# Differential attention on one core: the softmax, the transposes and the weighted sums of two tiles built as one pair

## The chip, the core and the metric

The kernel runs on one NeuronCore of a Trainium2 chip. The metric is the time of one execution in device microseconds (us); several executions are timed and the median is given. One further execution was recorded by the profiler, with its own time. The engines are named as in the profile: PE is TensorE, PEld its weight loads, DVE is VectorE, ACT is ScalarE, POOL is GpSimd, and SP issues most of the DMA transfers.

## The reference, cut to what matters

Two layers are applied to two independent requests of 512 tokens (x_prompt and x_sample, 1024 wide), each as x + mixer(RMSNorm(x)), and a last RMSNorm closes. Layer 1 is differential attention with 8 heads, layer 2 a bidirectional retention. The change lies in the attention of layer 1:

```
def block(qi):
    s = jnp.einsum('bqhd,bkhd->bhqk', qi, k).astype(f32)
    p = jax.nn.softmax(s, axis=-1).reshape(B, N_HEADS, 2, Q_BLOCK, S)
    a = (p[:, :, 0] - lam * p[:, :, 1]).astype(v.dtype)
    return jnp.einsum('bhqk,bkhe->bqhe', a, v)
...
o = rms_norm(o, subln_g, SUBLN_EPS) * (1.0 - lambda_init)
o = o.reshape(B, S, D_INNER) * jax.nn.silu(gate)
return o @ w_out
```

Each head has two score matrices, two softmaxes whose difference weighs the values (256 wide), a norm over the 256 columns, a gate, and the output projection to 1024 columns.

## The kernel before

All products are done in three passes over a high and a low part of each operand (`PASSES`), so one logical product is three matmuls. The program has four stages: the input projection of layer 1 (to about 617 us in the profile), the attention and its output projection (to about 1003 us), the input projection of layer 2 (to about 1480 us), and the retention with its output projection.

**Who sets the order.** The program text does not issue instructions. Each helper (`pe`, `act`, `dve`, `pool`, `axpy`, `dma`, `evac`) puts an operation on a `Plan` with a cost and with what it reads and writes. At the end `Plan.issue` lists the operations for all engines eight times with assumed costs and keeps the shortest plan. PE takes ready operations by their place in the last round's PE order, no further than 24 places ahead (`WINDOW`); the other engines take them by a due time computed backwards from PE. So the program text sets the first order and which buffers are taken in turn, the plan sets the rest, and a change in one stage can also move instructions in another.

**The attention, tile by tile.** A tile is (head, request, 128 queries): 64 tiles, numbered i, four to each head and request. For each tile:

- `scores` (L1202): two banks `sc`, three matmuls of 128x512 each.
- `row_max` (L1210): DVE takes the negated maximum of each bank.
- `exps` (L1220): ACT writes the exponentials into `p` and their sums into `sm`. When both are read the `sc` banks are free.
- `combine` (L1230 to L1239): POOL computes the factor of the second softmax (for the first four tiles DVE does), DVE forms the difference in place (L1236); on odd tiles POOL squares the sums of both tiles.
- `transp` (L1247): four 128x128 transposes into the only `tp` bank, a high part by ACT (L419) and a low part by DVE (L422) into the `aT` of the tile pair.
- `av` (L1267), once for two tiles: 24 matmuls of 128x256 into one of two `o` banks; then `weigh`: the gate (DVE L862), high and low part (L419, L422), the square (ACT L866) and the sum of its halves (DVE L867).
- `weighed`, once for two tiles: `norm_cols` transposes the squares (PE L874), sums them (ACT L878) and has POOL form the norm factor `rr` (L1279, L882). It owes four output pieces (`owe`).
- An output piece, `out_step` (L950, L955): six matmuls of 128x512 into one of three `pj` banks, and an `axpy` on DVE that scales by `rr` and adds to `xN`. The owed pieces wait in the list `todo`; `fill(n, lag)` puts up to n of them on the plan and leaves the last `lag` (`LAG` is 4) in the list. The weights of the pieces are split into parts twice for each head (L419 and L422 on 128x1024).

The loop before runs over single tiles: odd tiles start with an output piece and the weighted sum of the pair that ended two tiles ago, then come scores, softmax, an output piece, the transposes of the tile before, another piece, and on even tiles `weighed`.

Of the kernel before, what the change touches and what calls it, by code (L numbers as in the profile page):

```python
# [20 lines left out]
NH = 8  # L21
# [12 lines left out]
LAG = 4  # L34
# [221 lines left out]
def trunk_kernel(  # L256
# [15 lines left out]
    pj = ctx.enter_context(tc.tile_pool(name="pj", bufs=1, space=bass.MemoryType.PSUM))  # L272
# [8 lines left out]
    def view(pool, tag, i, size, shape, dt=F32):  # L281


        n = math.prod(shape[1:])
        if (tag, i) not in places:
            if size <= 32 and pool in (cp, wk):
                k = next(k for k, used in enumerate(gaps) if used + size <= PAD - 32)
                places[tag, i] = pads[k][:, gaps[k]:gaps[k] + size]
                gaps[k] += size
            else:  # L290
                places[tag, i] = pool.tile([P, size], F32, tag=f"{tag}{i}", name=f"{tag}_{i}", bufs=1)
        t = places[tag, i][0:shape[0], 0:n]
# [21 lines left out]
    def slot(n, shape, dt=F32R, shift=0):  # L314

        size = math.prod(shape[1:])
        at = None if n in (12, 13) or n >= 20 else n if n < 12 else n - 2
        if at is None:  # L320
            assert not shift
            cnt[0] += 1
            label = f"b_{cnt[0]}"
            return Buf(plan, f"b{n}", 1, lambda i: cp.tile(shape, dt, tag=f"b{n}", name=label))
        assert dt == F32R
        lo = at * 1024 + shift

        def make(i):
            t = arena[:, lo:lo + size]
            return t.rearrange("p (a b) -> p a b", a=shape[1]) if len(shape) == 3 else t  # L330
        b = Buf(plan, f"b{n}", 1, make)
        b.also = Buf(plan, f"edge{at + 1 if shift else at}", 1, None)
        return b
# [38 lines left out]
    def bank(tag, name=None):  # L372
        return Buf(plan, tag, BUFS[tag], lambda i: view(pj if tag == "pj" else sc, tag, i, S, [P, S]))
# [8 lines left out]
    def step(gen, n=1):  # L382
        for _ in range(n):
            next(gen, None)
# [24 lines left out]
    def pe(cost, fn, r, w, wait=0.0):  # L409
        plan.op("PE", cost, fn, r, w, wait=wait)  # L410
# [7 lines left out]
    def hi_of(n, dst, src, r, w):  # L418
        act(n, lambda: nc.scalar.copy(dst(), src()), r, w)  # L419

    def lo_of(n, dst, src, hi, r, w):
        dve(n, lambda: nc.vector.tensor_tensor(dst(), src(), hi().bitcast(F32), op=ALU.subtract), r, w)  # L422
# [409 lines left out]
    def projections(units, early):  # L832

        n = 2 + len(early)
        for u, place in zip(units[2:], early):
            u.early = place
        order = product_order(units, n)
        ready = 0
        for n, (u, op) in enumerate(order):
            while ready < len(order):  # L840
                v, p = order[ready]
                if sum(w.n_ws for w, _ in order[n:ready]) + v.n_ws > WS_BUFS:
                    break
                v.prep(p)
                ready += 1
            if units is first_units and n == len(order) - 1:
                u.product(op, 0)
                yield
                u.product(op, 1)
            else:  # L850
                u.product(op)
            u.evac(op)
            yield
# [34 lines left out]
    def load_qk(src, i, shift):  # L888
        t = slot(i, [P, 2, S], F32R, shift)
        dma(lambda: t.t.bitcast(F32), lambda: src[0][src[1]], [src[0]], [t], 512)  # L890
        return t

    def load_v(src, i, shift):
        out = []
        for a in range(2):
            t = slot(i + a, [P, NT, 256], F32R, shift)
            dma(lambda a=a, t=t: t.t.bitcast(F32), lambda a=a: src[a].rearrange("p (t e) -> p t e", t=NT),
                [src], [t], 512)
            out.append(t)
        return out  # L900

    def load_sg(src):
        t = os_t(F32, "sg")
        dma(lambda: t.t, lambda: src[:], [src], [t], 512)
        return t
# [5 lines left out]
    def fill(n, lag=0):  # L911
        for _ in range(n):
            if len(todo) > lag:
                todo.pop(0)()

    def new_xN(g, src):
        for t in range(NT):
            x = xN[g, t] = slot(20 + 4 * g + t, [P, D], F32)
            dma(lambda x=x: x.t, lambda t=t: src(t)[0], src(t)[1], [x], 512)
# [197 lines left out]
    for t in range(NT):  # L1117
        x_norm(0, t)
        x = xnat[0, t]
        half, at = t // 2, t % 2 * P  # L1120

        def turns(x=x, half=half, at=at):
            for k in range(4):
                lo = k % 2 * 256 + at
                nc.tensor.transpose(turned[half][k // 2][:, lo:lo + P], x[:, k * P:(k + 1) * P], ident.t)
        pe(0.44, turns, [ident, (x, 0)], [(ps, t) for ps in turned[half]])
        if half == 0:
            warm_up(2 if t else 1, [(x, 0)])
        if t % 2:
            for k in range(4):  # L1130
                first_piece(k, half)
# [3 lines left out]
    proj = projections(first_units, (12, 20, 22))  # L1135
# [41 lines left out]
    tiles = [(h, g, t) for h in range(NH) for g in range(NG) for t in range(NT)]  # L1177
    N = len(tiles)
# [3 lines left out]
    def fetch1(h, g, v=True):  # L1182
        for j in range(2):
            for which in range(2):
                qk[h, g, j, which] = load_qk((qk_d[0, which, h, g], j), 6 * which + 2 * g + j, 64 * which)
        if v:
            fetch1_v(h, g)

    def fetch1_v(h, g):
        vt[h, g] = load_v(v_d[0, h, g], 10 + 4 * g, 64)  # L1190
        sg[h, g] = load_sg(g_d[0, h, g])
# [48 lines left out]

    def transp(i):
        p, n = st[i]['p'], i % 2
        tp = bank("tp", "tpa")

        def fn():
            for j in range(NT):
                nc.tensor.transpose(tp[:, j * P:(j + 1) * P], p[:, 0, j * P:(j + 1) * P], ident.t)  # L1247
        pe(0.44, fn, [p, ident], [tp])
        if n == 0:
            st[i]['aT'] = [slot(4 + u, [P, NT, 256], F32R, 28) for u in range(2)]  # L1250
        aT, here = st[i - n]['aT'], slice(n * P, (n + 1) * P)
        src = lambda: tp.t.rearrange("p (j n) -> p j n", j=NT)
        hi_of(S, lambda: aT[0][:, :, here], src, [tp], [(aT[0], n)])
        lo_of(S, lambda: aT[1][:, :, here], src, lambda: aT[0][:, :, here], [tp, (aT[0], n)], [(aT[1], n)])
# [29 lines left out]
    def finished(g, t, i, half, n, key, end):  # L1284
# [11 lines left out]
        if (g, t) == (1, 1):  # L1296
            for place, n in ((2, 8),):
                todo[place:place] = [lambda: step(made, 1)] * n

    def at(f, i, n):  # L1300
        if 0 <= i < n:
            f(i)
# [3 lines left out]
    turns2 = itertools.chain(["sc", "o", "sc", "o"], itertools.cycle(["tp", "o"]))  # L1306
    made = make_b(1, x_source(1, xN, lambda g: next(turns2) if g else "pj"))

    for i in range(N + 5):
        if i % 2 and i > 2:  # L1310
            fill(1, LAG)
            at(av, i - 3, N)
        at(scores, i, N)
        at(row_max, i, N)
        at(exps, i, N)
        at(combine, i, N)
        if i < 5:
            step(proj, 1)
            if i in (2, 4):
                new_xN(i // 2 - 1, lambda t, g=i // 2 - 1: (xs[g][0, t * P:(t + 1) * P, :], []))  # L1320
            if i == 3:
                fetch1_v(0, 1)
        if not i % 2 or i < 3:
            fill(1, LAG)
        at(transp, i - 1, N)
        fill(1, LAG)
        if i % 2 == 0 and i > 3:
            at(weighed, i - 4, N)
        if i < N and i % 4 == 2 and i > 4:
            nh, ng = tiles[i][0:2]  # L1330
            if ng == 1 and nh + 1 < NH:
                fetch1(nh + 1, 0)
            elif ng == 0 and nh > 0:
                fetch1(nh, 1)
    while todo:
        fill(1)

# [5 lines left out]
    proj = projections(second_units, (12, 20, 22))  # L1343
# [275 lines left out]
```

## Time and profile before

| | |
|---|---|
| timed executions | 1798.52, 1798.78, 1799.33 us; median 1798.78 |
| profiled execution | 1797.39 us, of which the span from first to last instruction is 1795.2 |
| busy in the span | PE 1784.5, PEld 1562.0, DVE 1482.9, ACT 897.9, POOL 156.4 us |
| mean granted clock of TensorE | 0.999 |
| moved by DMA | 328.81 MB, 183 GB/s over the span |

The profiled execution is 1.39 us below the median of the timed ones. A busy time is the sum of an engine's instructions; those of PE overlap, so its pace is read from starts. Times of rows count from the start of the span.

### The profile page before, as it was taken

To read this page: it belongs to the slowest core of one execution; us is meant where nothing else is said; L and a number is where in the kernel's file an instruction comes from. 1 tells how busy PE (TensorE), PEld (TensorE's weight loads), DVE (VectorE), ACT (ScalarE), POOL (GpSimd) and SP (SyncE) were. 2 spreads that over 40 slices of the span, in tenths; PEclk is the share of its full clock that TensorE was granted. 3 is DMA by queue.
4 is the path that set the end of the run, shared out by engine and by line. 5 is a ranking of instruction groups with operands and counts; after the bars stand their busy time and mean duration, and the time that the engine had idled before them with its cause. 6 is when DMAs were issued, how large, how long until landed. Compare 5 with 4: busy or idle time off the path is not lost.

```text
span 1795.2 us, 27855 instructions
## 1 busy us (share of the span) xinstructions
PE 1784.5 (99%) x10321; PEld 1562.0 (87%) x10321; DVE 1482.9 (83%) x2340; ACT 897.9 (50%) x1865; POOL 156.4 (9%) x315
## 2 busy tenths in 40 slices
PE   9999999999999999999999999999999999999998
PEld 7889889898988888888888888898989988888887
DVE  8968788778699888888888897777887967888887
ACT  8754344343443565455555876444444454444446
POOL 1000000000000022222222200000000000111113
PEclk9999999999999999999999999999999999999999
DMA  6444554555545695454454524465647459664652
GB/s 219 141 136 141 165 163 148 191 162 153 187 124 183 209 336 200 161 186 169 168 181 140 200 71 142 141 211 164 210 137 240 142 191 409 260 230 176 232 213 94
DMA packets 162767, 328.81 MB, mean 183 GB/s; under 512 B 12724, under 2 KB 76872, under 8 KB 162632
## 3 DMA queue, kind: packets, MB, share of 16 engines
q1 hardware_dynamic: 162304, 326.71, 53.4%
q8 instruction: 81, 1.33, 0.3%
q14 instruction: 54, 0.44, 0.1%
q10 hardware_dynamic: 328, 0.34, 0.1%
HBM read 209.55 MB, written 117.44 MB: 182 GB/s over the span
## 4 chain that ended last, share of the span: by engine, by line
PE 95%; DVE 3%; ACT 1%; DMA 1%; issue 0%; POOL 0%; POOLq 0%; ACTq 0%; DVEq 0%
PE pj L637 21%; PE pj L950 19%; PE sc L637 11%; PE pj L647 10%; PE o L637 8%; PE o L1267 5%; PE sc L1202 5%; PE sc L647 5%; PE o L1444 2%; PE o L647 2%; PE tp L1247 2%; PE sc L1400 1%; PE tp L1424 1%; PE o L1452 1%; DVE ws L422 1%
## 5 line engine op out<-in xcount | busy, mean ns | idle before, releaser
L950 PE MATMUL pj<-ws,arena 128*128 128x512 f32 x1542 | 388.5, 395 | 0.0
L950 PEld LDWEIGHTS pj<-ws,arena 128*128 128x128 f32 x1542 | 277.6, 188 | 50.9 <-ACT m L404 0.2
L637 PE MATMUL pj<-b,ws 128*128 128x512 f32 x1080 | 263.3, 390 | 0.5 <-DVE e L698 0.5
L637 PEld LDWEIGHTS pj<-b,ws 128*128 128x128 f32 x1080 | 201.2, 188 | 42.2 <-issue 0.9
L955 DVE SCALAR_TENSOR_TENSOR b<-pj,pad,b 128x512 f32<-128x512 f32 (+1 forms) x257 | 190.2, 745 | 18.8 <-PE pj L950 17.9
L422 DVE TENSOR_TENSOR ws<-st,ws 128x512 fp32r<-128x512 f32 (+1 forms) x192 | 148.0, 775 | 63.2 <-ACT ws L419 56.4
L419 ACT CAST ws<-st 128x512 fp32r<-128x512 f32 (+1 forms) x192 | 132.0, 692 | 130.6 <-PE pj L637 41.9
L422 DVE TENSOR_TENSOR ws<-raw,ws 128x512 fp32r<-128x512 f32 (+2 forms) x165 | 142.0, 864 | 65.8 <-ACT ws L419 56.8
L637 PE MATMUL sc<-arena,ws 128*128 128x512 f32 x768 | 185.2, 389 | 0.0
L637 PE MATMUL o<-arena,ws 128*128 128x512 f32 x744 | 178.1, 390 | 0.0
L419 ACT CAST ws<-raw 128x512 fp32r<-128x512 f32 (+2 forms) x165 | 125.9, 768 | 90.2 <-PE o L637 48.1
L637 PEld LDWEIGHTS sc<-arena,ws 128*128 128x128 f32 x768 | 143.9, 188 | 29.8
L637 PEld LDWEIGHTS o<-arena,ws 128*128 128x128 f32 x744 | 138.5, 188 | 28.6 <-DVE arena L484 0.3
L637 PE MATMUL pj<-arena,ws 128*128 128x512 f32 x636 | 156.2, 390 | 0.0
L637 PEld LDWEIGHTS pj<-arena,ws 128*128 128x128 f32 x636 | 118.5, 188 | 24.2
L1220 ACT ACTIVATE b<-sc,pad 128x512 f32<-128x512 f32 x128 | 88.1, 691 | 79.2 <-DVE pad L1210 78.2
L690 ACT COPY c<-pj 128x512 f32<-128x512 f32 x104 | 60.8, 586 | 122.9 <-PE pj L637 69.0
L647 PE MATMUL pj<-ws,b 128*128 128x256 f32 x960 | 116.9, 275 | 0.0
L647 PEld LDWEIGHTS pj<-ws,b 128*128 128x128 f32 x960 | 113.3, 188 | 0.6
L1202 PE MATMUL sc<-arena 128*128 128x512 f32 x384 | 102.1, 393 | 0.0
L1267 PEld LDWEIGHTS o<-arena 128*128 128x128 f32 x768 | 93.2, 188 | 2.6
L1267 PE MATMUL o<-arena 128*128 128x256 f32 x768 | 93.7, 277 | 0.0
(223 smaller groups left out, 2862.6 us busy)
## 6 DMA issues: line engine op xcount, KB each, us to landing
qk<-os SPq DMA_DIRECT2D x192, 256.0 KB, 3.5
arena<-qk SPq DMA_DIRECT2D x96, 512.0 KB, 5.2
raw<-in_da_w_in_dram SPq DMA_DIRECT2D x64, 512.0 KB, 5.1
v<-os SPq DMA_DIRECT2D x64, 512.0 KB, 4.9
arena<-v SPq DMA_DIRECT2D x64, 512.0 KB, 4.2
raw<-in_ret_w_in_dram SPq DMA_DIRECT2D x48, 512.0 KB, 4.5
os<-g SPq DMA_DIRECT2D x32, 512.0 KB, 7.7
g<-e SPq DMA_DIRECT2D x48, 256.0 KB, 5.6
```

The lines of the kernel that those rows point to most:

```text
L419: act(n, lambda: nc.scalar.copy(dst(), src()), r, w)
L422: dve(n, lambda: nc.vector.tensor_tensor(dst(), src(), hi().bitcast(F32), op=ALU.subtract), r, w)
L637: nc.tensor.matmul(ps.t, a[u][0]()[:, k, :], bt[k][:, v, :], start=(opens and k == 0 and i == 0), stop=(k == 3 and i == 2), skip_group_che ...
L647: nc.tensor.matmul(ps[:, (t % 2) * 256:(t % 2) * 256 + 256], bt[k][:, v, t * P:(t + 1) * P], a[u][0]()[:, k, :], start=(opens and t % 2 == ...
L690: act(S, lambda c=c, ps=ps: nc.scalar.copy(c.t, ps.t), [ps], [c])
L950: nc.tensor.matmul(ps[:, here], o[a][:, e, t * P:(t + 1) * P], u[b][:, e, here], start=(m == 0), stop=(m == 5))
L955: axpy(n, lambda half=half, here=here, ps=ps: nc.vector.scalar_tensor_tensor(half, ps[:, here], rr[:, t % 2:t % 2 + 1], half, op0=ALU.mult ...
L1202: nc.tensor.matmul(s.t, q[:, a, t * P:(t + 1) * P], k[:, b, :], start=(n == 0), stop=(n == 2))
L1220: act(840, lambda j=j, s=s, m=m: nc.scalar.activation(p[:, j, :], s.t, AF.Exp, bias=m.t, accum_out=sm[:, 2 * j + n:2 * j + n + 1]), [s, m] ...
L1247: nc.tensor.transpose(tp[:, j * P:(j + 1) * P], p[:, 0, j * P:(j + 1) * P], ident.t)
L1267: nc.tensor.matmul(o[:, e * 256:(e + 1) * 256], v[b][:, j, e * P:(e + 1) * P], aT[a][:, j, :], start=(n == 0), stop=(n % 12 == 11), skip_g ...
L1444: nc.tensor.matmul(o[:, e * 256:(e + 1) * 256], v_[v][:, 2 * c + j, e * P:(e + 1) * P], a_[:, u, j * 256:(j + 1) * 256], start=(e == 0 and ...
```

## The change

It touches `transp` and the loop over the tiles. Tiles 0 to 5 keep the order of before. From tile 6 on the loop takes two tiles at once: scores and softmax of the even tile, two output pieces, scores and softmax of the odd tile, two output pieces, the weighted sum of the pair before, the transposes of both tiles behind each other, then the transposes of the squares of an earlier pair. The transposes of odd tiles go to a `pj` bank, which the output pieces use too. How many pieces stay in the list rises from 0 at tile 10 to 4 at tile 18. The counts of projection steps in the first five tiles are 1, 1, 2, 1, 0 in place of five times 1. Loads for the next head are put on the plan at the same tiles as before, at the end of the pair. No instruction is added or left out.

```
     def transp(i):
         p, n = st[i]['p'], i % 2
-        tp = bank("tp", "tpa")
+        tp = bank("pj" if n else "tp", "tpa")
...
+    FIRST = 6
...
-    for i in range(N + 5):
-        if i % 2 and i > 2:
-            fill(1, LAG)
-            at(av, i - 3, N)
+    def soften(i):
         at(scores, i, N)
         at(row_max, i, N)
         at(exps, i, N)
         at(combine, i, N)
...
+    GIVE = {0: 1, 1: 1, 2: 2, 3: 1}
...
+    for i in range(FIRST, N + 4, 2):
+        soften(i)
+        lag = max(0, min(LAG, i // 2 - 5))
+        fill(2, lag)
+        if i == FIRST:
+            transp(i - 1)
+        soften(i + 1)
+        fill(2, lag)
+        at(av, i - 2, N)
+        at(transp, i, N)
+        at(transp, i + 1, N)
+        at(weighed, i - 4, N)
+        fetch_next(i)
```

What the plan makes of it on PE, from a weighted sum (L1267) on, in the middle of the attention. Before, in the names `sc`, `o`, `tp` and `pj` are banks with their number, `b` the softmax tile that is transposed, `m` a square, `ws` output weights:

```order
L1267 MATMUL o_1_332<-arena_72 128x256 x24
L1202 MATMUL sc_0_248<-arena_72 128x512 x3
L1202 MATMUL sc_1_329<-arena_72 128x512 x3
L1247 MATMUL tp_0_293<-ident_0_240,b_43_5777 128x128 x4
L950 MATMUL pj_1_341<-ws_2_77,arena_72 128x512
L950 MATMUL pj_1_341<-ws_3_79,arena_72 128x512
```

And the same place after:

```order
L1267 MATMUL o_1_332<-arena_72 128x256 x24
L1247 MATMUL tp_0_293<-ident_0_240,b_43_5799 128x128 x4
L1247 MATMUL pj_0_289<-ident_0_240,b_44_5832 128x128 x4
L874 MATMUL o_0_296<-ident_0_240,m_1_441 128x128 x2
L1202 MATMUL sc_0_248<-arena_72 128x512 x3
L1202 MATMUL sc_1_329<-arena_72 128x512 x3
L950 MATMUL pj_1_341<-ws_0_73,arena_72 128x512
L950 MATMUL pj_1_341<-ws_1_75,arena_72 128x512
```

The two runs of transposes of a pair have become one run of ten behind the weighted sum; behind it follow in a fixed round six score matmuls, twelve of two output pieces, six of scores, twelve of two pieces, and the next weighted sum.

On DVE, from the gate of a weighted sum (L862) on; `c` is the gated sum, `pad` holds maxima and factors, `arena` the parts for PE. Before:

```order
L862 TENSOR_TENSOR c_1_514<-o_0_296,os_1_367 128x512
L1210 TENSOR_REDUCE pad_1_76<-sc_1_329 128x1
L867 TENSOR_TENSOR m_3_466<-m_3_466 128x256
L422 TENSOR_TENSOR arena_72<-tp_0_293,arena_72 128x4x128
L955 SCALAR_TENSOR_TENSOR b_36_228<-pj_1_341,pad_2_78,b_36_228 128x512
L1210 TENSOR_REDUCE pad_1_76<-sc_0_248 128x1
L422 TENSOR_TENSOR arena_72<-c_1_514,arena_72 128x2x256
L1236 SCALAR_TENSOR_TENSOR b_62_6830<-b_62_6830,pad_1_76 128x512
```

After:

```order
L862 TENSOR_TENSOR c_2_522<-o_1_332,os_2_607 128x512
L422 TENSOR_TENSOR arena_72<-tp_0_293,arena_72 128x4x128
L422 TENSOR_TENSOR arena_72<-pj_1_341,arena_72 128x4x128
L1210 TENSOR_REDUCE pad_1_76<-sc_0_248 128x1
L1210 TENSOR_REDUCE pad_1_76<-sc_1_329 128x1
L867 TENSOR_TENSOR m_0_251<-m_0_251 128x256
L955 SCALAR_TENSOR_TENSOR b_28_222<-pj_2_410,pad_2_78,b_28_222 128x512
L422 TENSOR_TENSOR arena_72<-c_2_522,arena_72 128x2x256
L955 SCALAR_TENSOR_TENSOR b_28_222<-pj_0_289,pad_2_78,b_28_222 128x512
L1210 TENSOR_REDUCE pad_1_76<-sc_0_248 128x1
L1236 SCALAR_TENSOR_TENSOR b_65_6970<-b_65_6970,pad_1_76 128x512
L1210 TENSOR_REDUCE pad_1_76<-sc_1_329 128x1
```

The low parts of both transposed tiles now stand together ahead of the first pair of maxima; the first combination of a pair (L1236) stands between the maxima of the second, and the list ends with two axpys and the second combination before the next gate.

A third place lies at the very start, where the plan's choice changed although the program text there did not: PE's first transposes of the fourth token tile (`b_4`; L1125 takes its first half, L1098 its second). Before:

```order
L658 MATMUL pj_1_341<-arena_72,ws_0_73 128x256 x3
L1098 MATMUL sc_0_248<-ident_0_240,b_1_244 128x128
L1098 MATMUL sc_0_248<-ident_0_240,b_2_253 128x128
L1098 MATMUL sc_0_248<-ident_0_240,b_3_257 128x128
L1098 MATMUL sc_0_248<-ident_0_240,b_4_261 128x128
L1125 MATMUL sc_1_329<-ident_0_240,b_4_261 128x128 x2
L1125 MATMUL o_1_332<-ident_0_240,b_4_261 128x128 x2
L658 MATMUL pj_1_341<-arena_72,ws_0_73 128x256 x9
```

After:

```order
L658 MATMUL pj_1_341<-arena_72,ws_0_73 128x256 x3
L1125 MATMUL sc_1_329<-ident_0_240,b_4_261 128x128 x2
L1125 MATMUL o_1_332<-ident_0_240,b_4_261 128x128 x2
L1098 MATMUL sc_0_248<-ident_0_240,b_1_244 128x128
L1098 MATMUL sc_0_248<-ident_0_240,b_2_253 128x128
L1098 MATMUL sc_0_248<-ident_0_240,b_3_257 128x128
L1098 MATMUL sc_0_248<-ident_0_240,b_4_261 128x128
L658 MATMUL pj_1_341<-arena_72,ws_0_73 128x256 x9
```

The four L1125 transposes moved ahead of the four of L1098; further on, three matmuls of L637 that stood between two groups of L658 stand behind them.

More of the change, by code (lines that the diff above doesn't have):

```diff
@@ L1316, in trunk_kernel, with leave @@
         at(combine, i, N)
+    def leave(i):
+        step(proj, GIVE.get(i, 0))
         if i < 5:
-            step(proj, 1)
             if i in (2, 4):
@@ L1322, in trunk_kernel, with fetch_next @@
                 fetch1_v(0, 1)
+    GIVE = {0: 1, 1: 1, 2: 2, 3: 1}
+    def fetch_next(i):
+        if i < N and i % 4 == 2 and i > 4:
+            nh, ng = tiles[i][0:2]
+            if ng == 1 and nh + 1 < NH:
+                fetch1(nh + 1, 0)
+            elif ng == 0 and nh > 0:
+                fetch1(nh, 1)
+    for i in range(FIRST):
+        if i % 2 and i > 2:
+            fill(1, LAG)
+            at(av, i - 3, N)
+        soften(i)
+        leave(i)
         if not i % 2 or i < 3:
@@ L1328, in trunk_kernel @@
             at(weighed, i - 4, N)
[L1329 to L1334, printed above, removed]
+        fetch_next(i)
+    for i in range(FIRST, N + 4, 2):
+        soften(i)
+        lag = max(0, min(LAG, i // 2 - 5))
[8 more added lines that the diff above has]
+        at(weighed, i - 4, N)
+        fetch_next(i)
     while todo:
```

## The prediction

> **What bounds the kernel now.** I read the page first, then who PE waited for, then the attention stage by windows and by a timeline of PE, then a timeline of the other engines there.
>
> ```profile
> PE 1784.5 (99%) x10321; PEld 1562.0 (87%) x10321; DVE 1482.9 (83%) x2340; ACT 897.9 (50%) x1865; POOL 156.4 (9%) x315
> PE sc L1075 <- DVE pad L431: 1.2, 1, 1.2
> PE sc L1098 <- ACT b L404: 1.0, 1, 1.0
> ...
> 800.00:840.00 40.00, 40.00 (x227) 34.60 (x227) 33.70 (x53) 21.48 (x56) 10.39 (x24) 1.00 0.53 186
> ```
>
> PE is busy for 1784.5 of 1795.2 us. The longest wait in its list is 1.2 us, and none of the rows is a line of the attention. The last row is 40 us out of its middle: PE 40.00, DVE 33.70, ACT 21.48, POOL 10.39 us, clock 1.00. So the stage runs at PE's pace, and a new order can gain only what PE loses between its instructions, while it can lose whatever wait it brings. Busy time cannot show the pace, because matmuls overlap; the starts can:
>
> ```profile
> 805.07 0.60 PE L1247 MATMUL tp<-ident,b 128*128 128x128 f32 x4
> 805.50 0.38 PE L874 MATMUL o<-ident,m 128*128 128x128 f32 x2
> 805.64 1.63 PE L950 MATMUL pj<-ws,arena 128*128 128x512 f32 x6
> 807.11 2.94 PE L1267 MATMUL o<-arena 128*128 128x256 f32 x24
> 809.88 1.55 PE L1202 MATMUL sc<-arena 128*128 128x512 f32 x6
> 811.27 0.60 PE L1247 MATMUL tp<-ident,b 128*128 128x128 f32 x4
> 811.62 1.64 PE L950 MATMUL pj<-ws,arena 128*128 128x512 f32 x6
> 813.10 1.54 PE L1202 MATMUL sc<-arena 128*128 128x512 f32 x6
> 814.48 2.89 PE L950 MATMUL pj<-ws,arena 128*128 128x512 f32 x12
> 817.20 0.60 PE L1247 MATMUL tp<-ident,b 128*128 128x128 f32 x4
> ```
>
> From one L1247 to the same place a pair later, 805.07 to 817.20, a pair of tiles takes 12.13 us. Start to start the pieces are 0.43 (four transposes), 0.14 (two), 1.47, 2.77 (weighted sum), 1.39, 0.35, 1.48, 1.38 and 2.72 us. Twelve matmuls of 128x512 well behind the last transposes take 2.72 us, 1.36 for six, but six take 1.47 and 1.48 straight behind transposes, and 1.39 and 1.38 where scores follow the weighted sum or those pieces. A part of the surplus behind transposes is their own: the last of a run hands over early, since a run of four takes 0.35 us where it ends and 0.43 where another follows.
>
> **The change part by part.** *PE in a pair.* The matmuls are the same; only the neighbours change. By these rows a new pair is: eight transposes 2 x 0.43 = 0.86, two of squares 0.14, scores behind them 1.47, two pieces 2.72 + 0.02 (the rest of the slow stretch, as in 1.38 against 1.36), scores 1.36, two pieces 2.72, weighted sum 2.77: 12.06 us, 0.07 below 12.13. One slow stretch has gone, and one run end. The rows are rounded to 0.01 and the step from the weighted sum straight into transposes hardly stands in the trace, so I bound the gain by 0 (each change of shape costs as much wherever it stands) and 0.11 (the stretch ends with the first six matmuls and the run of ten hands over like two), and take 0.05. The loop has 29 such pairs (tiles 6 to 63): **-1.5 us, ends 0 and -3.2.**
>
> *Does PE find its inputs in time?* That is what a loss would come from. The durations, with starts that give the pitch between neighbours:
>
> ```profile
> 801.86 0.69 DVE L1210 TENSOR_REDUCE pad<-sc 128x1 f32<-128x512 f32 x1
> 802.47 0.68 DVE L422 TENSOR_TENSOR arena<-c,arena 128x512 fp32r<-128x512 f32 x1
> ...
> 803.07 0.75 DVE L1236 SCALAR_TENSOR_TENSOR b<-b,pad 128x512 f32<-128x512 f32 x1
> 803.73 0.69 DVE L1210 TENSOR_REDUCE pad<-sc 128x1 f32<-128x512 f32 x1
> 805.10 0.19 ACT L1220 ACTIVATION_READ_ACCUMULATOR b<-sc,pad 128x1 f32 x1
> 805.37 0.54 POOL L1230 TENSOR_TENSOR pad<-pad 128x1 f32<-128x1 f32 x1 [3.01 <-ACT b L1220]
> 805.70 0.59 ACT L419 CAST arena<-tp 128x512 fp32r<-128x512 f32 x1 [0.41 <-PE tp L1247]
> 806.01 0.34 POOL L1234 TENSOR_SCALAR pad<-pad 128x1 f32<-128x1 f32 x1
> 806.18 0.27 ACT L878 ACTIVATE o<-o 128x128 f32<-128x128 f32 x1
> 806.60 0.26 ACT L878 ACTIVATE o<-o 128x128 f32<-128x128 f32 x1
> 810.08 0.69 DVE L862 TENSOR_TENSOR c<-o,os 128x512 f32<-128x512 f32 x1 [1.75 <-PE o L1267]
> 810.78 1.38 DVE L1210 TENSOR_REDUCE pad<-sc 128x1 f32<-128x512 f32 x2
> 810.80 0.60 ACT L866 ACTIVATE m<-o 128x512 f32<-128x512 f32 x1 [3.83 <-DVE c L862]
> 811.30 0.61 ACT L419 CAST arena<-c 128x512 fp32r<-128x512 f32 x1
> 811.81 0.69 ACT L1220 ACTIVATE b<-sc,pad 128x512 f32<-128x512 f32 x1
> 812.48 0.69 ACT L1220 ACTIVATE b<-sc,pad 128x512 f32<-128x512 f32 x1
> 824.54 1.22 DVE L422 TENSOR_TENSOR ws<-raw,ws 128x1024 fp32r<-128x1024 f32 x1
> ```
>
> PE's end reaches DVE and ACT after 0.20 us (the weighted sum ends at 809.88, the gate starts at 810.08; the transposes at 805.50, the cast at 805.70). Set T = 0 at the first transpose of a new pair. PE then has the squares at 0.86, the first scores from 1.00 to 2.47, pieces to 5.21, the second scores to 6.57, pieces to 9.29, the weighted sum to 12.06.
>
> *First scores to second.* The second scores need the two `sc` banks at 5.21 and 5.89. ACT, in its new order: cast of the even tile at 0.63, of the odd at 1.11, the two sums of squares at 1.59 and 2.01, the square at 2.43, the cast of the gated sum at 2.93, the exponentials at 3.44 and 4.11 (pitches 0.48, 0.42, 0.50, 0.51, 0.67). DVE: gate 0.20, low parts 1.25 and 1.85 (pitch 0.60), first maximum when the second is written, 2.54, second 3.23 (two take 1.38), so the maxima are there at 3.23 and 3.92 and hold up neither exponential. These end at 4.13 and 4.80: **a reserve of 1.1 us**.
>
> *Second scores to the odd transposes at T = 12.06 + 0.43.* DVE goes on at 3.92 with the square sum, axpy, low part, and at 5.51 the second axpy; second maxima at 6.17 and 7.44 with the first combination between; the last exponential at 8.2 to 8.9, its sum read by 9.1, POOL 0.54 + 0.34 with two steps of 0.1 to 10.1, the second combination 10.2 to 10.9: a reserve of 1.5 us. In pairs where DVE splits output weights (1.22 us, ahead of the second maxima) everything behind moves by that, in part into DVE's gaps, and about 1.0 remains. DVE then idles to 12.26, when the weighted sum is done, much as now (1.75). The bank that odd transposes take from `pj` is read by DVE up to 2.54; the piece that uses it next starts at 6.57, two pieces later. So no wait: 0, and it stays 0 until these chains grow by about a microsecond.
>
> *Clock.* Ten transposes stand behind each other, 1.0 us. A far longer run is in the trace already, 32 of them:
>
> ```profile
> 1014.79 4.35 PE L1098 MATMUL pj<-ident,b 128*128 128x128 f32 x32
> 1019.06 3.02 PE L950 MATMUL pj<-ws,arena 128*128 128x512 f32 x12
> 1014.80:1019.00 4.20, 4.20 (x33) 3.32 (x31) 3.96 (x7) 4.09 (x10) 0.25 (x1) 1.00 1.00 344
> ```
>
> The granted clock is 1.00 through 4.20 us of transposes. [...]
>
> *The start.* The plan takes the fourth token tile's first half ahead of its second.
>
> ```profile
> 12.24 0.71 ACT L404 ACTIVATE b<-b,pad 128x512 f32<-128x512 f32 x1
> ...
> 13.00 0.44 PE L1125 MATMUL sc<-ident,b 128*128 128x128 f32 x2 [0.33 <-ACT b L404]
> ```
>
> Now L1125 waits for ACT until 12.95; in the new order it waits for DVE, and L1098 for ACT. That can bring the chain forward by at most ACT's 0.71; against it, matmuls of L637 no longer fill between the L658 groups, which can open a gap of about a microsecond. I take -0.3, ends -0.7 and +1.0.
>
> *The first tiles and the tail.* In tiles 6 to 11 no output pieces are held back, so an axpy on DVE can stand waiting for `rr`, and the maxima behind it wait too; SP's list there has the first loads of head 1 ahead of stores and of the gate of the second request, which they push back by some entries. The projection steps move by a place. PE's fill is the same products. I take +0.2, ends -0.2 and +1.0. In the tail the last weighted sum has four pieces before its squares' transposes in place of two: 0.
>
> Sum: -1.5 - 0.3 + 0.2 = **-1.6 us**. Against the profiled execution that is 1797.39 - 1.6 = 1795.8; it lies 1.39 below the median of the timed runs, and against that, which is what is compared, 1798.78 - 1.6 = **1797.2 us**. The ends add to -4.1 and +2.0: 1794.7 to 1800.8.
>
> **The rivals.** I take 0.2% (3.6 us, so 1795.2 to 1802.4) for what a measurement of this kernel tells from no change.
>
> *Slower: the second scores wait for the first exponentials.* Before, scores of a pair were spread over its 12.13 us; now only two pieces, 2.74 us, part the two groups that share the `sc` banks. If DVE comes to its first maxima 1.4 us later than in my walk (the gate, two low parts and two casts stand ahead of them, and a late axpy or weight split would add its 0.75 or 1.22), PE stands 0.3 us in each of 29 pairs: +8.7 - 1.6 = +7.1, 1805.9 us. It decides from a delay of 1.1 us on. For it: DVE is busy for 33.70 of 40 us and in order. Against it: the walk leaves the reserve, and DVE's own gap before the gate takes up a delay once a pair. Chance 0.14.
>
> *Faster: the slow stretches go almost whole.* Then -3.2 in the attention and -0.7 to -0.9 at the start and the first tiles: -4.1, 1794.7 us. For it: 1.36 for six is what the trace has once the stretch is over. Against it: every pair keeps one run of transposes and one weighted sum. Chance 0.13.
>
> [...] Chance 0.01.
>
> **How the numbers follow.** My forecast, PE's pace and nothing else, has 0.72. It gives the time, 1797.2 us. Its own range is 1794.7 to 1800.8; that holds nearly all of 0.72. Drawn down to 1794.0 the range takes in most of the faster case, about 0.1, and leaves out the slower ones, 0.15. Faster by over 0.2% is 0.13, slower by over 0.2% is 0.15 (0.14 and 0.01), and between them 0.72.
>
> **What would show it right or wrong.** In the profile after: PE's list of waits still without a line of the attention, or only with tenths in the first tiles; the timeline of a pair with one run of ten transposes and about 12.06 to 12.10 us from one run to the next; the exponentials of the first tile of a pair ended about a microsecond before the second scores start; the gate on DVE still waiting for PE. It is wrong if idle time of L1202 on ACT's L1220, or of L1247 on DVE's L1236, comes back in each pair; if the pair is above 12.2 us without any wait, the cost of changed shapes was misread; if it is below 12.0, the slow stretch was shorter than I took it.

## The result, and the profile after

The changed kernel takes 1795.75 us (median of 22 runs, 1794.85 to 1797.74) beside 1797.82 us of the kernel before (22 runs, 1795.40 to 1799.93). The ratio is 0.9988, 95% interval 0.9983 to 0.9994: a gain of 0.12%, which is real and lies within the 0.2% that the prediction took for no change. The profiled execution took 1795.28 us with a span of 1793.5, against 1797.39 and 1795.2. So 0.4 of the 2.1 us between the two lie outside the span from the first to the last instruction: time less span is 2.1 to 2.2 us in every run of the kernel before for which both are on record, and 1.7 to 1.9 in every one of the changed kernel. What makes that difference stays open.

From the page of the changed kernel, and from its list of what PE waited for (total, times, longest):

```profile
span 1793.5 us, 27921 instructions
PE 1783.2 (99%) x10321; PEld 1564.8 (87%) x10321; DVE 1483.4 (83%) x2341; ACT 893.5 (50%) x1864; POOL 168.0 (9%) x315
```

```profile
PE tp L1098 <- ACT os L404: 0.5, 1, 0.5
PE pj L1247 <- DVE b L1236: 0.4, 1, 0.4
```

PE is still the bound. One line of the attention has come into the list: odd transposes (L1247) wait once for a combination on DVE (L1236). The line of 1.0 us that the list had before, L1098 for ACT's L404, has gone. (The row of 0.5 us, L1098 for ACT's `os`, stands at 15.3 us, in the start of the program; the second profile of the changed kernel does not have it.) POOL, with the same work, is busy for 168.0 us in place of 156.4.

PE's timeline of one pair in the changed kernel:

```profile
810.79 0.60 PE L1247 MATMUL tp<-ident,b 128*128 128x128 f32 x4
811.22 0.60 PE L1247 MATMUL pj<-ident,b 128*128 128x128 f32 x4
811.66 0.38 PE L874 MATMUL o<-ident,m 128*128 128x128 f32 x2
811.80 1.63 PE L1202 MATMUL sc<-arena 128*128 128x512 f32 x6
813.26 2.89 PE L950 MATMUL pj<-ws,arena 128*128 128x512 f32 x12
815.99 1.52 PE L1202 MATMUL sc<-arena 128*128 128x512 f32 x6
817.35 2.88 PE L950 MATMUL pj<-ws,arena 128*128 128x512 f32 x12
820.07 2.92 PE L1267 MATMUL o<-arena 128*128 128x256 f32 x24
822.83 0.60 PE L1247 MATMUL tp<-ident,b 128*128 128x128 f32 x4
```

From 810.79 to 822.83 a pair takes 12.04 us (12.13 in the rows of the prediction). One pair is a sample; pairs before alternate between 12.08 and 12.13. So take 18 pairs, tile 20's transposes to tile 56's, with the same 432 pieces, 216 scores and 432 matmuls of the weighted sums in both. The first and last row before, then after:

```profile
738.65 0.60 PE L1247 MATMUL tp<-ident,b 128*128 128x128 f32 x4
956.55 0.60 PE L1247 MATMUL tp<-ident,b 128*128 128x128 f32 x4
```

```profile
738.55 0.60 PE L1247 MATMUL tp<-ident,b 128*128 128x128 f32 x4
955.27 0.60 PE L1247 MATMUL tp<-ident,b 128*128 128x128 f32 x4
```

217.90 us against 216.72: 12.105 and 12.040 us a pair, a gain of 0.065.

To split the time I cut each trace at two rows of PE's timeline: the first scores, and the 32 transposes with which layer 2 begins. For the changed kernel they are

```profile
619.93 0.84 PE L1202 MATMUL sc<-arena 128*128 128x512 f32 x3
1014.85 4.35 PE L1098 MATMUL pj<-ident,b 128*128 128x128 f32 x32
```

All profiles, in us (the last column is the span less the second row):

| kernel | first scores at | attention | layer 2 to the end |
|---|---|---|---|
| before | 619.16 | 395.63 | 780.4 |
| changed | 619.93 | 394.92 | 778.6 |
| changed, second profile (after_again) | 620.03 | 394.86 | 778.7 |
| e1_half | 621.39 | 397.54 | 778.7 |
| e2_extra_run | 619.41 | 395.62 | 779.0 |
| e4_bank | 619.49 | 399.41 | 778.7 |
| e5s_fill04 | 621.38 | 438.05 | 778.9 |
| e9_before_recip | 618.80 | 395.63 | 780.3 |
| e6_first8 | 620.08 | 395.39 | 778.7 |
| e7_lag4 | 619.39 | 396.32 | 779.4 |
| b2_first12 | 619.97 | 394.80 | 778.8 |
| b2_first8, two profiles | 620.75, 619.31 | 394.29, 394.59 | 778.9, 778.9 |
| b2_first6 | 619.89 | 394.36 | 779.7 |

Cut this way, the 1.7 us of span between the two kernels are -0.7 in the attention, -1.8 from the start of layer 2 on, and +0.8 ahead of the attention. The +0.8 is not the change's: six profiles that share the changed kernel's order of PE there reach their first scores between 619.41 and 621.38, and eight that share the old one between 618.80 and 621.39.

The largest part, then, lies where the prediction had put zero. Three timelines of the kernel before, around the start of layer 2 (DVE, POOL and ACT, PE):

```profile
1024.16 0.69 DVE L587 TENSOR_TENSOR st<-raw,raw 128x512 f32<-128x512 f32 x1
1024.76 1.89 DVE L422 TENSOR_TENSOR arena<-m,arena 128x512 fp32r<-128x512 f32 x3
1024.81 2.84 POOL L983 TENSOR_TENSOR pad<-pad,pad 128x1 f32<-128x1 f32 x1 [2.16 <-ACT pad L976]
1026.57 0.69 DVE L587 TENSOR_TENSOR st<-st,raw 128x512 f32<-128x512 f32 x1
1027.68 1.15 ACT L404 ACTIVATE b<-b,pad 128x1024 f32<-128x1024 f32 x1 [1.98 <-POOL pad L983]
1028.88 0.33 PE L1098 MATMUL sc<-ident,b 128*128 128x128 f32 x1 [1.03 <-ACT b L404]
```

And the same place in the changed kernel:

```profile
1023.58 2.50 DVE L422 TENSOR_TENSOR arena<-m,arena 128x512 fp32r<-128x512 f32 x4
1025.29 1.19 POOL L983 TENSOR_TENSOR pad<-pad,pad 128x1 f32<-128x1 f32 x1 [2.68 <-ACT pad L976]
1026.52 0.75 DVE L406 TENSOR_SCALAR b<-b,pad 128x1024 f32<-128x1024 f32 x1 [0.44 <-POOL pad L983]
1027.41 0.60 PE L1098 MATMUL sc<-ident,b 128*128 128x128 f32 x4
```

L983 is POOL's power that gives the last row its norm. Its other runs in the kernel before take 0.54 to 0.87 us; here it took 2.84 before and 1.19 after. In both it ends 0.39 to 0.40 us after DVE has come to the end of a stretch of operations with two inputs in SBUF (before 1026.57 + 0.69 = 1027.26 against 1027.65, after 1026.08 against 1026.48). The changed kernel starts this power 0.48 us later and ends it 1.17 us earlier, so nothing upstream had become faster: the new plan put less DVE work of that kind on top of it. It also gave the next step to DVE (0.75) and not to ACT (1.15). PE's wait of 1.0 us is gone. In each of the other eleven profiles in which POOL runs L983 the longest of its 16 takes 0.86 to 1.39 us, and PE does not wait for the row in any of them.

What the wait is worth, and what else is in the 1.8 us, PE's timeline shows. Before:

```profile
1027.36 0.49 PE L1098 MATMUL sc<-ident,b 128*128 128x128 f32 x3
1030.28 2.98 PE L637 MATMUL pj<-arena,ws 128*128 128x512 f32 x12
...
1042.06 3.01 PE L637 MATMUL sc<-arena,ws 128*128 128x512 f32 x12
1046.24 3.01 PE L637 MATMUL o<-arena,ws 128*128 128x512 f32 x12
...
1771.50 16.66 PE L950 MATMUL pj<-ws,arena 128*128 128x512 f32 x78
```

After, where the first of these places is the row of 1027.41 above:

```profile
1029.08 2.98 PE L637 MATMUL pj<-arena,ws 128*128 128x512 f32 x12
...
1040.85 3.01 PE L637 MATMUL sc<-arena,ws 128*128 128x512 f32 x12
1044.82 3.00 PE L637 MATMUL o<-arena,ws 128*128 128x512 f32 x12
...
1770.01 16.66 PE L950 MATMUL pj<-ws,arena 128*128 128x512 f32 x78
```

The transposes in which PE waits take 2.92 us before and 1.67 after: 1.25 of the 1.8. The next transposes of such rows, with the products ahead of them, take 4.18 and 3.97: another 0.2. From layer 2's first transposes to the last row it is 756.71 and 755.16 us, so 1.55 are there and almost all of it is gained by 1046 us. The last 0.2 lie behind PE's last matmul.

### The profile page after: what moved, and what is told of

It is laid out like the page before. It is cut to its first block, busy times and chain, and to the rows that moved or that the text cites. A ratio compares the mean times of both kernels' runs of the same rounds, so it can differ in the third digit from the quotient of the medians.

```text
span 1793.5 us, 27921 instructions
## 1 busy us (share of the span) xinstructions
PE 1783.2 (99%) x10321; PEld 1564.8 (87%) x10321; DVE 1483.4 (83%) x2341; ACT 893.5 (50%) x1864; POOL 168.0 (9%) x315
## 4 chain that ended last, share of the span: by engine, by line
PE 94%; DVE 4%; ACT 1%; issue 0%; POOL 0%; POOLq 0%; DVEq 0%; ACTq 0%
PE pj L637 20%; PE pj L950 19%; PE sc L637 11%; PE pj L647 10%; PE o L637 7%; PE sc L1202 5%; PE sc L647 5%; PE o L1267 5%; PE o L1470 2%; PE o L647 2%; PE sc L1426 1%; PE tp L1450 1%; PE o L1478 1%; DVE ws L422 1%; PE pj L1247 1%; PE tp L1247 1%
## 5 line engine op out<-in xcount | busy, mean ns | idle before, releaser
L950 PE MATMUL pj<-ws,arena 128*128 128x512 f32 x1542 | 378.1, 392 | 0.0
L950 PEld LDWEIGHTS pj<-ws,arena 128*128 128x128 f32 x1542 | 281.7, 188 | 54.7 <-DVE m L793 0.3
L637 PE MATMUL pj<-b,ws 128*128 128x512 f32 x1080 | 263.4, 390 | 0.5 <-DVE e L698 0.5
L637 PEld LDWEIGHTS pj<-b,ws 128*128 128x128 f32 x1080 | 201.1, 188 | 41.9 <-issue 0.9
L637 PE MATMUL sc<-arena,ws 128*128 128x512 f32 x768 | 185.2, 389 | 0.0
L637 PE MATMUL o<-arena,ws 128*128 128x512 f32 x744 | 178.1, 391 | 0.0
L637 PEld LDWEIGHTS sc<-arena,ws 128*128 128x128 f32 x768 | 144.0, 188 | 29.7
L637 PEld LDWEIGHTS o<-arena,ws 128*128 128x128 f32 x744 | 138.6, 188 | 28.6 <-DVE arena L484 0.3
L637 PE MATMUL pj<-arena,ws 128*128 128x512 f32 x636 | 156.1, 390 | 0.0
L637 PEld LDWEIGHTS pj<-arena,ws 128*128 128x128 f32 x636 | 118.6, 188 | 24.3
L1267 PEld LDWEIGHTS o<-arena 128*128 128x128 f32 x768 | 93.0, 188 | 2.5
L1267 PE MATMUL o<-arena 128*128 128x256 f32 x768 | 93.6, 277 | 0.0
```

Of the source, the lines that this page charges most:

```text
L637: nc.tensor.matmul(ps.t, a[u][0]()[:, k, :], bt[k][:, v, :], start=(opens and k == 0 and i == 0), stop=(k == 3 and i == 2), skip_group_che ...
L950: nc.tensor.matmul(ps[:, here], o[a][:, e, t * P:(t + 1) * P], u[b][:, e, here], start=(m == 0), stop=(m == 5))
L1267: nc.tensor.matmul(o[:, e * 256:(e + 1) * 256], v[b][:, j, e * P:(e + 1) * P], aT[a][:, j, :], start=(n == 0), stop=(n % 12 == 11), skip_g ...
```

## The experiments

All edits but those of e4 and e9 are made to the changed kernel. e1, e2, e4, e5s, e6 and e7 ran once each, so their totals say little and their rows decide; beside the first four the kernel before took 1799.08 us in its one run.

**e1_half: both orders in one trace.**

```diff
-    FIRST = 6
+    FIRST = 34
```

> Tiles up to 33 are built in the old order and the pairs from 34 on in the new one, so one trace holds both paces. Neighbours of PE's matmuls set the pace: a pair takes 12.13 us in the first half and 12.04 in the second, with no wait in either, and the attention's total lies between the two kernels'. If the gain came from something else than the order of the pairs (the plan of the start, the chip's condition, the layer's end), both halves take the same, 12.04 or 12.13. The start of this kernel stands in the old order and the end of the layer in the new one: if the wait of 1.0 us for ACT at the start of layer 2 belongs to the old end of the attention, it is absent here; if it belongs to the old start of the program or to chance, it may be here. Time of the run: about 1796 (1794.5 to 1797.5).

PE's transposes (L1247) at the ends of an old and of a new pair of this one trace:

```profile
743.54 0.60 PE L1247 MATMUL tp<-ident,b 128*128 128x128 f32 x4
755.66 0.60 PE L1247 MATMUL tp<-ident,b 128*128 128x128 f32 x4
911.19 0.60 PE L1247 MATMUL tp<-ident,b 128*128 128x128 f32 x4
923.23 0.60 PE L1247 MATMUL tp<-ident,b 128*128 128x128 f32 x4
```

12.12 and 12.04 us: the pace goes with the order of the pair, not with the run. The time was 1799.37 us, above the expected range. The attention takes 397.54, 2.6 more than in the changed kernel, with waits in its first tiles (1.0 us of scores for exponentials, 0.5 of the squares' transposes); the rest is about the 14 pairs more at 12.12 in place of 12.04. The wait at the start of layer 2 is absent.

**e2_extra_run: one run of transposes more.**

```diff
-    for i in range(FIRST, N + 4, 2):
+    for i in range(FIRST, N + 6, 2):
...
-        fill(2, lag)
+        fill(1, lag)
+        if i > FIRST:
+            at(weighed, i - 6, N)
+        fill(1, lag)
...
-        at(weighed, i - 4, N)
```

> The new order, but the two transposes of the squares stand by themselves between two output pieces, half a pair later, so that each pair again has two runs of transposes and two stretches behind them. If a run of transposes with the slow matmuls behind it is what a pair saved, the pair goes from 12.04 back to about 12.13 us, with no wait, and the time to about 1797.9. If the saving lay in the scores standing together or in the bank, the pair stays at 12.04 to 12.06 and the time at 1795 to 1796.

The first and last row of the same 18 pairs:

```profile
736.26 0.60 PE L1247 MATMUL tp<-ident,b 128*128 128x128 f32 x4
953.94 0.60 PE L1247 MATMUL tp<-ident,b 128*128 128x128 f32 x4
```

217.68 us, 12.093 a pair: of the 0.065 that a pair had gained, 0.053 are lost again by two transposes set apart, with the scores still together and the bank still the new one, and no line of the attention in PE's list of waits. The theory of the runs holds for most of the gain; the other 0.012 stay open. The time, 1795.74, is below the 1797.9 expected: I had priced the run at 0.09, from one pair, and in this order the wait of 0.4 in the first tiles is absent. The attention, 395.62, is 0.7 longer than in the changed kernel.

**e4_bank: the bank alone, in the kernel before.**

```diff
-        tp = bank("tp", "tpa")
+        tp = bank("pj" if n else "tp", "tpa")
```

> The kernel before with one edit, the odd tile's transposes in a bank of the pieces. By the theory of neighbours the bank alone changes nothing: a pair 12.13 us, the time 1797.4 within 1.5. If the bank were the gain, a pair would be at 12.04 to 12.06 and the time about 1795. The end of the layer is in the old order: if the wait of 1.0 us at the start of layer 2 belongs to that, it is here too.

```profile
740.76 0.60 PE L1247 MATMUL tp<-ident,b 128*128 128x128 f32 x4
958.92 0.60 PE L1247 MATMUL tp<-ident,b 128*128 128x128 f32 x4
```

218.16 us for the 18 pairs, 12.120 a pair: the bank brings nothing to the pace. The time, 1799.72, is above the expected 1797.4 within 1.5, for the plan came out worse in the first and last tiles: a wait of 1.3 us of L1247 for L1236 (at 1000.4 us) and one of 0.6 of scores for exponentials (at 643.5), and an attention of 399.41. The wait at the start of layer 2 is absent although the end of the attention is in the old order. So that wait does not belong to the old order as such.

**e5s_fill04: the reserve of the second scores.** All four pieces behind the second scores, with PE held to that order in tiles 14 to 61 (the lines of the plan that hold it are not shown).

```diff
-        fill(2, lag)
+        fill(0 if 14 <= i < N - 2 else 2, lag)
...
-        fill(2, lag)
+        fill(4 if 14 <= i < N - 2 else 2, lag)
```

> The new order with all four pieces of a pair behind its second scores and none between the two groups of scores, in the pairs from tile 14 on, which PE then issues in just that order (24 pairs). It measures the reserve on which the rival of the prediction rests. The trace of the changed kernel has the exponentials ended 1.22 us before the second scores start; two pieces are 2.73 us, so PE should wait 1.5 us in each of the pairs for the first exponentials (L1202 on ACT's L1220), a pair 13.55 us, the time about 1795.5 + 36 = 1831. By the reserve of 1.1 us worked out ahead of the run the wait is 1.6 and the time 1834. If the other engines catch up during the wait (maxima and exponentials earlier in the next pair), it is under 1 us a pair and the time below 1820; if nothing waits, the reserve was not one, and the time stays at 1796.

From this kernel's list of PE's waits, then from PE's timeline:

```profile
PE sc L1202 <- ACT b L1220: 35.3, 24, 1.5
```

```profile
802.51 0.60 PE L1247 MATMUL tp<-ident,b 128*128 128x128 f32 x4
...
803.52 1.63 PE L1202 MATMUL sc<-arena 128*128 128x512 f32 x6
806.63 1.66 PE L1202 MATMUL sc<-arena 128*128 128x512 f32 x6 [1.48 <-ACT b L1220]
808.13 5.61 PE L950 MATMUL pj<-ws,arena 128*128 128x512 f32 x24
...
816.33 0.60 PE L1247 MATMUL tp<-ident,b 128*128 128x128 f32 x4
```

PE waits in each of the 24 pairs. Six scores behind transposes take 1.46 us (811.80 to 813.26 above), so these are through at 804.98, and the second start 1.65 later. With two pieces, 2.73 us, between them that is a reserve of 1.08: the 1.1 of the prediction. A pair takes 13.82 us, not 13.55, since the scores behind the wait take 1.50 in place of 1.36 (806.63 to 808.13): PE is slow for a stretch behind an idle time too. The time was 1840.09 us, above every expectation by that and by a late start (621.38). The rival that was to make the kernel slower is thus a real mechanism at the price it was given; the two pieces keep it away.

**e9_before_recip: POOL out of the row's norm, in the kernel before.**

```diff
-        pool(200, lambda: nc.gpsimd.tensor_tensor(r.t, ss.t, mhalf[:, 0:1], op=ALU.pow), [ss, mhalf], [r])
+        dve(2, lambda: nc.vector.reciprocal(r.t, ss.t), [ss], [r])
```

> The kernel before, in which the norm of a finished row no longer goes through POOL's power: DVE takes a plain reciprocal instead (so the square root is left out, and the output is not the reference's). In the kernel before, POOL's last power ahead of layer 2 (L983) takes 2.84 us, where it takes 0.54 elsewhere; it ends 0.39 us after DVE's last operation with two inputs in SBUF, and PE then waits 1.03 us for the row (L1098 on ACT's L404). If POOL is held by DVE and that makes the wait, the wait is absent here and the part from layer 2's first transposes to the end, 780.4 us in the kernel before and 778.6 to 778.9 in the five others that ran, is 778.6 to 779.0; the attention stays in its old form, a pair 12.13 us; the time is 1.0 to 1.8 below the kernel before on the same chip (ratio 0.9990 to 0.9994). If the wait comes from the old end of the attention (last weighted sum 2.9 us later), it stays and the part stays at 780.4, the ratio at 1.0000.

DVE and ACT, then PE, at the start of layer 2:

```profile
1024.43 0.16 DVE L983 RECIPROCAL pad<-pad 128x1 f32<-128x1 f32 x1
1024.69 1.18 ACT L404 ACTIVATE b<-b,pad 128x1024 f32<-128x1024 f32 x1
1026.93 0.60 PE L1098 MATMUL sc<-ident,b 128*128 128x128 f32 x4
1027.37 0.60 PE L1098 MATMUL o<-ident,b 128*128 128x128 f32 x4
```

With the attention in its old form and its old length (395.63), the row leaves its norm at 1024.59 and no longer at 1027.65, L404 starts at once, and PE goes through. That settles the wait: it came from POOL's step, not from the end of the attention. (That DVE's operations had stretched this step is read from the traces, in the last section; no run took them away.) The total does not settle what it is worth: ratio 0.9995, interval 0.9986 to 1.0004, and 780.3 us from layer 2 on, not 778.6 to 779.0. This plan lost the time again further on. From layer 2's transposes to an output piece early in the retention it takes 485.48 us (1014.43 to 1499.91) where the kernel before takes 487.40 (1014.79 to 1502.19), so 1.9 are saved; then it loses 0.45 and 0.3 at two products of the retention (L1424, at 1501 and 1510), 0.6 in the last output pieces and about 0.5 behind them.

**The first tiles: e6, e7 and the three b2 kernels.** e6_first8 lets the new pairs begin at tile 8, e7_lag4 holds four pieces back from the start. The b2 kernels take tiles 0 to FIRST - 1 from the kernel before, with their bank and projection steps:

```diff
# e6_first8
-    FIRST = 6
+    FIRST = 8
# e7_lag4
-        lag = max(0, min(LAG, i // 2 - 5))
+        lag = LAG
# b2: FIRST = 6, 8 or 12, and
-        tp = bank("pj" if n else "tp", "tpa")
+        tp = bank("pj" if n and i >= FIRST else "tp", "tpa")
-    GIVE = {0: 1, 1: 1, 2: 2, 3: 1}
+    GIVE = {0: 1, 1: 1, 2: 1, 3: 1, 4: 1}
```

> The new order from tile 8 on instead of tile 6. In the changed kernel the first tiles lose 1.2 us against its own later pace: a wait of 0.4 for a DVE combination at 694.8, and 0.1 to 0.3 at three places before 653. If the early start of pairs is what makes these, one of them or more goes: the attention takes 393.9 to 394.5 us instead of 394.9, at a cost of 0.08 for the one pair more in the old order, and nothing else moves. If they come from the first pieces, which are not there yet in either order, the attention takes 394.9 or a little more.

> The new order with four pieces held back from the first pair on, instead of none in tiles 6 to 11 and one more in every pair after. The prediction had the first tiles at +0.2 us because an axpy on DVE can stand waiting for the norm when no piece is held back. By that the wait of 0.4 for DVE's combination goes, and the attention takes 0.4 to 0.7 less than 394.9. Against it: held pieces leave PE with less to do between the first scores and the second, so that PE waits for the exponentials, 1.6 us where no piece stands between them; then the attention takes 396 us or more.

> Made from the runs so far: tiles 0 to 11 exactly as in the kernel before (old order, the odd transposes in the old bank, one step of the projection after each of the first five tiles), and the new pairs, with their bank, from tile 12 on. In before the first sixth of the attention loses 0.9 us over the pace of its matmuls, in the changed kernel 1.2 and another 0.7 in the wait behind tile 10. If those belong to the new order, the bank or the steps in the first tiles, they go, and the attention takes 393.6 to 394.2 us in place of 394.9 (before 395.6); with the start of layer 2 as in the changed kernel the time is 0.5 to 1.3 below the changed kernel's and 2.5 to 3.3 below before: ratio 0.9982 to 0.9988. If the first tiles lose whatever way the pairs are entered, the attention takes 394.9 and the ratio is that of the changed kernel, 0.9988.

> The changed kernel once more, beside the one before it in this list on the same chip. Its attention is 394.9 us within 0.1 again (the part in which PE goes through without a start or an end of the program); the wait of 0.4 us for DVE's combination stands at the same place if the order makes it, and not if it was chance. The start up to the first scores, 619.9 us in the one profile, 619.4 and 621.4 in two kernels with the same order there, varies by up to 2 us: it is no part of the change. Ratio 0.9988, between 0.9982 and 0.9994.

> As the kernel with the new pairs from tile 12 on, but from tile 8 on. It tells where the loss of the first tiles begins. If it is the bank and the steps of the projection in tiles 0 to 5, the attention takes 393.5 to 394.0 us here as well (two pairs more in the new order, 0.16 less); if it is the order of the pairs of tiles 8 to 11, where the first pieces stand, the attention takes 394.5 or more.

> The kernel with old tiles 0 to 7 and the new pairs from tile 8 on once more, now timed: its attention took 394.3 us in one look, 0.6 less than the changed kernel's 394.9 in two profiles, and the other parts are the changed kernel's. The time is 0.6 below the changed kernel's and 2.7 to 3.0 below before: ratio 0.9983 to 0.9986, against 0.9988 and 0.9989 of the changed kernel. If the one look was luck, the attention is at 394.7 or more in this profile and the ratio at 0.9988.

> The new pairs from tile 6 on as in the changed kernel, but with the old bank and the old steps of the projection in tiles 0 to 5. If these two make the loss of the first tiles, the attention takes 394.2 to 394.4 us (one pair more in the new order than from tile 8 on, 0.08 less, and the wait of 0.4 behind tile 10 may come back); if the early pairs make it, the attention takes 394.8 or more.

e6 (1795.98 us) takes the wait behind tile 10 away and gets two others in the first tiles (0.5 and 0.2): attention 395.39, worse. e7 (1796.86) goes the way its rival had it: two waits of 0.7 for exponentials and one of 0.3 for DVE's combination, attention 396.32. The prediction's reading that held-back pieces would help is not borne out.

The changed kernel again: ratio 0.9989 (0.9980 to 0.9998), attention 394.86, the wait of 0.4 in its place. So that wait comes from the order, not from chance.

With the old bank and steps in tiles 0 to 5, b2_first6 has an attention of 394.36, 0.5 less, and keeps the wait behind tile 10; its ratio is 0.9987 (0.9978 to 0.9996). From tile 8 on it is 394.29 and 394.59 in two profiles, and b2_first8 is the fastest kernel that ran: 1794.59 us, ratio 0.9983 (0.9975 to 0.9992), though its interval overlaps that of the changed kernel. b2_first12, whose PE goes through the first tiles in the order of before, gets a wait of 0.5 there that before has not (DVE and ACT are planned anew; b2_first8 has it too, with 0.2 and 0.4 in its two profiles): attention 394.80, above the 393.6 to 394.2 expected; ratio 0.9985 (0.9976 to 0.9993). About half of what the first tiles lose in the changed kernel, 0.5 of 1.2, goes away with the bank and the steps there, which no run took apart; two profiles of b2_first8 differ by 0.3, so the share is rough. Which waits arise in them beyond that changes with every plan.

## Why the prediction was right, and where it was not

The forecast was 1.6 us less than before, within 0.2%; measured is 2.1 less in the medians. The level, 1797.2 against 1795.75, is further off, since the median of before shown ahead of the change, 1798.78 of three runs, became 1797.82 with 22. But the sum came out near in part by luck. Measured, its terms are -1.9 for the pairs, +1.2 for the first tiles, -1.8 behind the attention, +0.8 for the start and -0.4 outside the span, together -2.1; only the first was forecast at about its size, and the others happen nearly to cancel:

- **PE in a pair: right in kind, sized a little low.** Worked out 0.07, taken 0.05, measured 0.065 over 18 pairs. (The one pair it was worked out from, 12.13, is the longest of the alternation; the mean is 12.105.) At 29 pairs that is -1.9, not -1.5. The pair itself came out at 12.04, under the 12.06 to 12.10 that I had named. e2 shows that a run of transposes with what stands behind it is most of what was saved, 0.053.
- **First scores to second: right.** A reserve of 1.1, measured 1.08 in e5s; in the pair shown above the second exponential of the first tile ends at 815.44 us, 1.2 before its bank is written again. The waits behind it never arose.
- **Odd transposes: the reserve holds, but not from the first pair on.** Worked out 1.5; in the pair shown the second combination ends at 821.68 us, 1.6 before the odd transposes at 823.26. In the first tiles a wait of 0.4 came.
- **The first tiles: mis-sized.** Taken +0.2, upper end +1.0; the attention's -0.7 less the pairs' -1.9 leaves +1.2. I had looked only at pieces not held back, and e7 shows that holding them back is worse. About half of it went away with the old bank, which I had put at nothing throughout, and the old steps of the projection.
- **The tail and what stands behind it: the step that failed.** "In the tail the last weighted sum has four pieces before its squares' transposes in place of two: 0." The sum has no term at all for what comes behind it, and from layer 2 on the profile has -1.8, more than the attention. The plan decides anew what stands where on DVE, far from the edited lines, and a wait of 1.0 us that my own first fence showed depended on that.
- **The start:** -0.3 taken; +0.8 in the one pair of profiles, inside what equal orders differ by, so neither right nor wrong.
- **The clock:** ten transposes behind each other left it at 1.00, as the row of 32 (1.00 through 4.20 us) had let expect. The 0.01 in the chance of slower was for a clock that falls behind the ten; no run shows a fall, and the mean clock of every run on record is 0.998 or more.

```profile
800.00:840.00 40.00, 40.00 (x229) 35.03 (x228) 33.78 (x53) 22.11 (x61) 11.03 (x24) 1.00 0.45 163
```

What stays open: what makes the 0.2 us behind PE's last matmul and the 0.4 outside the span; what each of bank and steps does in the first tiles; and why the time before varies more from run to run (1795.4 to 1799.9) than after.

## What to carry to other kernels

Where PE is the bound and never waits, count its changes of shape and its runs of transposes: a run less was worth 0.053 us a pair here (e2), and only the number of pairs makes it show. Where a planner sets the order, an edit in one stage re-deals the others; every short wait in the list of before is then at stake, and should have a price in the sum. And look at an operation whose time varies (0.54 to 2.84 us for one column) before calling its engine off the path.

## What the runs showed of the hardware

POOL's powers of one column took up to 1.48 us in place of 0.54 in the attention of the changed kernel when they began while DVE was reading two inputs from SBUF. Two rows of the changed kernel's DVE and POOL timelines, then the same operation while DVE runs nothing:

```profile
699.18 0.68 DVE L422 TENSOR_TENSOR arena<-c,arena 128x512 fp32r<-128x512 f32 x1
699.21 1.04 POOL L1230 TENSOR_TENSOR pad<-pad,pad 128x1 f32<-128x1 f32 x1 [1.36 <-ACT b L1220]
...
703.44 0.54 POOL L1230 TENSOR_TENSOR pad<-pad,pad 128x1 f32<-128x1 f32 x1 [2.74 <-ACT b L1220]
```

The longer one ends 0.39 us after DVE's. Counted over the changed kernel's trace, the 38 of POOL's powers (L983, L1230) that began under such a DVE operation took 0.84 to 1.48 us, and the 38 others 0.54 to 0.56; 15 of these began under an axpy alone (0.54 to 0.55) and one under a low part whose source is in PSUM (0.55). In the row of such DVE operations at the start of layer 2 the power lasts to the end of the row: 2.84 us before and 1.19 after, with the ends 0.39 and 0.40 after DVE's last. The sixty powers of L1230 take 32.9 us before and 51.0 after, which is more than the 11.6 us by which POOL's busy time grew. I had not priced it.

PE's slow stretch, 1.46 to 1.50 us for six matmuls that take 1.36 otherwise, follows PE's wait in e5s (1.48 us in the row, 1.50 for the six behind it) as well as a run of transposes (1.46 to 1.48); a smaller surplus follows a change of shape without either (1.39 us for six scores behind the weighted sum, in the rows of the prediction). What makes it no run here shows.
